# Two seven-product stages: four early quads run in pairs, and the second operand sum moved into the last head

## The chip, the cores and the metric

One core of one Trainium2 chip runs the whole program in one launch. The metric is device time in microseconds (us): the median of three runs of the kernel before is 1768.44 us (1766.1 to 1769.79). The trace is of a fourth execution of its own.

## The reference

One layer of a diffusion block on 1024 latent tokens of width 1024, with 256 context tokens, in float32. Two of its products carry the change: the latents times `w_in`, and the feed-forward's first product.

```python
h_lat = rmsnorm(x, norm1_g) * (1 + sc1) + sh1
u, v, q, k, vv, r, af, ab, ga, gb = split(h_lat @ w_in)
b_lat = gla(q, k, vv, af, ab, state of the context) normed * silu(r)   # 4 heads, forwards and backwards
a_lat = gelu(u) * (w_spatial mixing of layernorm(gelu(v)))
y = sigmoid(ga) * (a_lat @ w_branch_a) + sigmoid(gb) * (b_lat @ w_branch_b)
x = x + g1 * (y @ w_out)
h2 = rmsnorm(x, norm2_g) * (1 + sc2) + sh2
a, g = split(h2 @ w_ffn_in)
x = x + g2 * ((silu(g) * a) @ w_ffn_out)
return rmsnorm(x, final_norm_g)
```

## The kernel before, in words

**Products.** Every float32 operand is split into a high part (a cast on ACT to the reduced format fp32r) and a low part (raw minus high, on DVE). A product of two such operands is three matmuls of the parts (high by high, high by low, low by high) for each of its k blocks; `PASS` holds that order.

**Seven-product stages.** Blocks of columns of `w_in` (gb, u, r, ga) and of `w_ffn_in` are computed by a seven-product scheme on 2x2 blocks. The moving operands (tokens) are the blocks B11, B21, B22 and four sums T1 to T4 of blocks, computed once for a stage; the stationary ones (weights) are A11, A12, A22 and the sums S1 to S4. One **quad** is two column blocks of 128 for all 1024 tokens: seven products of 12 matmuls of 128x512, in the order A11 by B11 and A12 by B21 (`ahead_1`, `ahead_2`), then S3 by T3, S2 by T2, S1 by T1, A22 by T4, S4 by B22 (`others`). S3 and S2 accumulate in PSUM bank X, and A22 after them; S1 and S4 in bank Y. Between S3 and S2 ACT copies X into `q7` (L736), and the next product into X waits for that copy. After S2 DVE forms `u3` (L741), GpSimd subtracts `q7` from it (L742), DVE adds Y into `u3` (L744), and so on; `sink` applies the activation and stores. The latent stage has 16 quads, the feed-forward stage 22.

**Early quads.** `early_quads` runs the first two products of some quads before the sums T exist: they need only A11, A12, B11 and B21. In the latent stage these are quads 0 to 3 inside the last head (from `between`, which also forms T3 in `h_first`), and quads 4 and 5 after the head; in the feed-forward stage quads 0 to 3. Then `h_others` (latents) or `other_operands` (feed-forward) forms the sums on DVE, with the weights of quad 0 split between T2 and T1, and `run_quads` goes quad by quad: `weights_s` of one quad, then its five products.

**Weights.** `weights` (L689) loads one column block as a tile `wr` of 512 KB by a DMA from SyncE. `wr` comes from the pool `wraw`, which has 3 buffers, so a fourth load waits for the last reader of the first:

```python
wraw = ctx.enter_context(tc.tile_pool(name="wraw", bufs=3))
```

`weights_s` reads both column blocks (va, ga) of a quad: S3 = A11 - A21 (L700), S2 = A22 - S3 (L701), S1 = S2 + A11 (L702), S4 = A12 - S2 (L703, the last reader of va), splits S3 and S2 as one tile, S1 and S4 as another (`parts_of`, L637 cast, L638 low part), and splits A22 (L709, L710, the last reader of ga). In early quads L702 and L703 are on DVE, in later ones on GpSimd. The split of a first weight goes through `split_w` (L236 cast, L237 low part) and the pool `wspl` of 4 buffers.

**Order.** Each engine runs its queue strictly in order. A scheduler fixes the queues when the program is built; `pe` chains the matmuls of these stages in program order, so that PE never passes a product that waits.

**The last head.** `head` computes scores and masks, then for each of four pairs of chunks `outputs`: matmuls, a sum of squares on ACT, `rstd` (DVE L171, GpSimd L172), a scaling on ACT (L596); one step later `outputs_T`: four transposes on PE (L605) and two copies on DVE (L610).

## Time and profile before

| | us |
|---|---|
| median of three runs (lowest to highest) | 1768.44 (1766.1 to 1769.79) |
| profiled execution: its own time | 1771.97 |
| profiled execution: span from first to last instruction | 1770.2 |
| PE busy in the span | 1712.4 (97%) |
| DVE busy | 1138.8 (64%) |
| ACT busy | 668.5 (38%) |
| POOL (GpSimd) busy | 215.4 (12%) |

The profile gives busy time by engine, the time that each engine stood idle and what ended it, and the TensorE clock that was granted (1.00 is 2.4 GHz, 0.50 is 1.2 GHz). A matmul's row lasts 0.39 us, but the matmuls of a product overlap: the distance between two starts counts. The latent stage's stretch is 396 to 741 us, the feed-forward's 1108 to 1550 us.

### The profile page before, as it was taken

The numbers are of one execution on the slowest core, as the hardware profiler recorded it, in microseconds if no ns is written. First come the engines' busy times: TensorE is split into PE (matmuls) and PEld (weight loads), VectorE is DVE, ScalarE is ACT, GpSimd is POOL, SyncE is SP. The second block draws the span as 40 slices with busy tenths as digits, with TensorE's granted clock in tenths as the row PEclk, the third lists the DMA queues.
The fourth block names the chain that finished last, engine by engine and source line by source line (L and its number), as shares of the span: only waits on it lengthen the run. The fifth ranks groups of instructions, "written<-read, shape, count | busy, mean of one in ns | idle before, by whom it ended". The sixth has DMA issues, their size and how long they took to land.

```text
span 1770.2 us, 21603 instructions
## 1 busy us (share of the span) xinstructions
PE 1712.4 (97%) x8162; PEld 1407.5 (80%) x8162; DVE 1138.8 (64%) x1559; ACT 668.5 (38%) x974; POOL 215.4 (12%) x193
## 2 busy tenths in 40 slices
PE   8899999999899999999999999989999999999997
PEld 3887888888678888877888888768888888888886
DVE  7686595867865464277656745885545555466797
ACT  6663423323443434234322213533333333355343
POOL 2220000000112353000000000012122122000001
PEclk9999999999999999999999999989999999999999
DMA  9511234052354454387858951233222232377572
GB/s 339 156 37 36 85 118 179 24 179 60 113 155 133 129 179 125 124 293 260 262 190 308 321 191 74 70 116 98 77 90 83 75 92 84 127 242 277 180 270 99
DMA packets 219961, 267.89 MB, mean 151 GB/s; under 512 B 11920, under 2 KB 142032, under 8 KB 219856
## 3 DMA queue, kind: packets, MB, share of 16 engines
q1 hardware_dynamic: 219040, 265.08, 45.1%
q0 software_dynamic: 720, 1.40, 0.2%
q8 instruction: 64, 1.05, 0.2%
q14 instruction: 41, 0.34, 0.1%
q10 hardware_dynamic: 96, 0.02, 0.0%
HBM read 205.64 MB, written 60.82 MB: 151 GB/s over the span
## 4 chain that ended last, share of the span: by engine, by line
PE 79%; DVE 11%; DMA 4%; issue 3%; ACT 3%; POOL 1%; SPq 0%; DVEq 0%; ACTq 0%; POOLq 0%
PE m L716 20%; PE g L716 17%; PE m L273 13%; PE m L1283 5%; PE g L1283 5%; PE m L1166 5%; PE m L285 4%; PE g L538 2%; DVE s L638 1%; PE m L822 1%; DVE wlo L237 1%; DVE s L422 1%; PE g L822 1%; DMA s<-in_w_ada_dram 1%; PE g L1363 1%
## 5 line engine op out<-in xcount | busy, mean ns | idle before, releaser
L716 PE MATMUL m<-s,s 128*128 128x512 f32 x1320 | 313.5, 395 | 8.8 <-ACT q L736 3.8
L716 PEld LDWEIGHTS m<-s,s 128*128 128x128 f32 x1320 | 251.0, 191 | 65.1 <-ACT q L736 5.8
L273 PE MATMUL m<-s,whi 128*128 128x512 f32 (+1 forms) x832 | 252.3, 384 | 2.2 <-ACT s L990 1.5
L237 DVE TENSOR_TENSOR wlo<-wr,whi 128x1024 fp32r<-128x1024 f32 x92 | 112.4, 1224 | 194.2 <-ACT whi L236 194.0
L716 PE MATMUL g<-s,s 128*128 128x512 f32 x960 | 225.0, 391 | 9.0 <-ACT q L736 4.1
L716 PEld LDWEIGHTS g<-s,s 128*128 128x128 f32 x960 | 179.2, 188 | 51.6 <-ACT q L736 6.6
L273 PEld LDWEIGHTS m<-s,whi 128*128 128x128 f32 x832 | 154.0, 188 | 33.2 <-ACT s L990 2.4
L236 ACT CAST whi<-wr 128x1024 fp32r<-128x1024 f32 x92 | 96.5, 1051 | 214.1 <-PE m L273 107.9
L273 PE MATMUL m<-s,wlo 128*128 128x512 f32 (+1 forms) x416 | 158.9, 383 | 1.8 <-DVE wlo L237 1.8
L637 ACT CAST s<-s 128x1024 fp32r<-128x1024 f32 x98 | 102.4, 1052 | 134.4 <-DVE s L638 62.2
L638 DVE TENSOR_TENSOR s<-s,s 128x1024 fp32r<-128x1024 f32 x98 | 145.4, 1494 | 9.9 <-ACT s L637 6.0
L172 POOL TENSOR_TENSOR rstd<-rstd,nhalf 128x1 f32<-128x1 f32 (+2 forms) x43 | 29.1, 678 | 847.7 <-DVE rstd L171 847.6
L285 PE MATMUL m<-whi,s 128*128 128x256 f32 x640 | 126.0, 291 | 0.1
L716 PE MATMUL g<-s,whi 128*128 128x512 f32 x384 | 118.5, 390 | 0.0
L638 DVE TENSOR_TENSOR s<-wr,s 128x1024 fp32r<-128x1024 f32 x77 | 92.3, 1233 | 22.8 <-ACT s L637 22.1
L285 PEld LDWEIGHTS m<-whi,s 128*128 128x128 f32 x640 | 101.5, 192 | 4.2 <-issue 2.7
L742 POOL TENSOR_TENSOR q<-u,q 128x512 f32<-128x512 f32 x38 | 59.4, 1563 | 314.1 <-DVE u L741 150.3
L637 ACT CAST s<-wr 128x1024 fp32r<-128x1024 f32 x77 | 78.2, 1053 | 49.9 <-DMA wr<-wsT 25.3
L285 PE MATMUL m<-wlo,s 128*128 128x256 f32 x320 | 92.3, 289 | 2.6 <-DVE wlo L237 1.9
L273 PEld LDWEIGHTS m<-s,wlo 128*128 128x128 f32 x416 | 78.3, 188 | 16.6 <-DVE wlo L237 2.0
L1166 PE MATMUL m<-s,s 128*128 128x512 f32 x384 | 87.6, 390 | 0.0
L1166 PEld LDWEIGHTS m<-s,s 128*128 128x128 f32 x384 | 72.0, 188 | 14.9
(293 smaller groups left out, 2879.2 us busy)
## 6 DMA issues: line engine op xcount, KB each, us to landing
wr<-in_w_in_dram SPq DMA_DIRECT2D x82, 512.0 KB
s<-in_w_ada_dram SPq DMA_DIRECT2D x48, 512.0 KB
wr<-in_w_ffn_in_dram SPq DMA_DIRECT2D x48, 512.0 KB
wr<-actd SPq DMA_DIRECT2D x77, 256.0 KB
s<-in_w_ffn_out_dram SPq DMA_DIRECT2D x22, 512.0 KB
wsT<-s SPq DMA_DIRECT2D x44, 256.0 KB
wr<-wsT SPq DMA_DIRECT2D x44, 256.0 KB
wr<-in_w_ffn_out_dram SPq DMA_DIRECT2D x33, 256.0 KB
```

Source lines behind the costliest of these rows:

```text
L236: nc.scalar.copy(hi, raw)
L237: lo_sub[0] = nc.vector.tensor_sub(lo, raw, f(hi)).ins
L273: nc.tensor.matmul(ps, ws[a][:, k, :], get(b, k, t0, n), start=k == 0 and i == 0, stop=k == nk - 1 and i == 2)
L285: nc.tensor.matmul(ps[:, j, :], get(b, 4 * kh + k, (2 * tp + j) * P, P), ws[a][:, k, :], start=kh == 0 and j == 0 and k == 0 and i == 0, s ...
L538: r = nc.tensor.matmul(pkv[:, j, :], kt[:, j, :], vt(n), start=j == 0, stop=True, skip_group_check=True)
L637: nc.scalar.copy(hi, raw)
L638: nc.vector.tensor_sub(lo, raw, f(hi))
L716: pe(nc.tensor.matmul(ps, wts[a][:, k, :], mov[k // 2][b][:, k % 2, :], start=start and k == 0 and i == 0, stop=k == 3 and i == 2, skip_gr ...
L742: nc.gpsimd.tensor_sub(q7, u3, q7)
L822: pe(nc.tensor.matmul(banks[tt], op[mov][kp][b][:, kk, tt * P:(tt + 1) * P], wts[a][:, kk, :], start=start and kp == 0 and kk == 0 and i = ...
L1166: pe(nc.tensor.matmul(ps, yF.get(b, k, tt * P, P), wo[k // 2][a][:, k % 2, :], start=k == 0 and i == 0, stop=k == KT - 1 and i == 2))
L1283: pe(nc.tensor.matmul(banks[tt], o[b][:, 0, tt * P:(tt + 1) * P], o[a][:, 1, :], start=start and k == 0 and i == 0, stop=k == KH - 1 and i ...
```

## The change

Five things are changed. (1) `quad_pair` takes quads 0 and 1 together, then 2 and 3: the weights of both first, then each of the five products for both quads before the next product, with 4 PSUM banks for their X and Y. (2) In the latent stage quads 4 and 5 are no longer early: they run as every later quad does. (3) `weights_s` is a generator that splits S1 and S4 later, after S2's products; with GpSimd the sums S1, S4 come before the split of S3 and S2. (4) The sums T are a generator as well (`h_sums`, `f_sums`), stepped between the products of the first pair; T2 of the latents is formed in steps after each `outputs` of the last head, and the sums are formed in place. (5) T4 of the latents subtracts the tile that now holds T2.

```diff
@@ -616,6 +616,7 @@
                 outputs_T(jp - 1, ons[jp - 1])
+            step()
         for fo in range(2):
@@ -667,18 +668,27 @@
-    def other_operands(op, blk, after):
+    def in_place(op, dst, xs, ys):
+        for d, a, b in zip(dst, xs, ys):
+            getattr(nc.vector, op)(d, a, b)
+    def f_sums(op, blk):
...
-        dve = (nc.vector, nc.vector)
-        t3 = combined("tensor_sub", b22, b12, dve)
-        op["T3"] = moving(t3)
-        t2 = combined("tensor_add", t3, b11, dve)
-        op["T2"] = moving(t2)
-        after()
-        op["T1"] = moving(combined("tensor_sub", b12, b11, dve))
-        op["T4"] = moving(combined("tensor_sub", b21, t2, dve))
+        t = combined("tensor_sub", b22, b12, (nc.vector, nc.vector))
+        op["T3"] = moving(t)
+        yield
+        in_place("tensor_add", t, t, b11)
+        op["T2"] = moving(t)
+        yield
+        in_place("tensor_sub", b12, b12, b11)
+        op["T1"] = moving(b12)
+        yield
+        in_place("tensor_sub", b21, b21, t)
+        op["T4"] = moving(b21)
+        yield
...
+        yield
@@ -695,20 +705,38 @@
-        nc.vector.tensor_sub(s32[:, 0], a11, a21)
-        nc.vector.tensor_sub(s32[:, 1], a22, s32[:, 0])
-        eng.tensor_add(s14[:, 0], s32[:, 1], a11)
-        eng.tensor_sub(s14[:, 1], a12, s32[:, 1])
-        for t, names in ((s32, ("S3", "S2")), (s14, ("S1", "S4"))):
+        def split(t, names):
...
+        def sums14():
+            eng.tensor_add(s14[:, 0], s32[:, 1], a11)
+            eng.tensor_sub(s14[:, 1], a12, s32[:, 1])
+        nc.vector.tensor_sub(s32[:, 0], a11, a21)
+        nc.vector.tensor_sub(s32[:, 1], a22, s32[:, 0])
+        if eng is nc.gpsimd:
+            sums14()
+        split(s32, ("S3", "S2"))
+        if eng is nc.vector:
+            sums14()
...
+        yield
+        split(s14, ("S1", "S4"))
+        yield
+    def whole(*gens):
+        for _ in zip(*gens):
+            pass
@@ -761,19 +794,33 @@
-    def run_quads(op, todo, quads, hook=None):
+    def quad_pair(op, todo, quads, at, sums=None):
+        ws = [weights_s(*weights(*todo[at + i][:2]), quads[at + i]["ops"], nc.vector) for i in range(2)]
+        steps = [others(quads[at + i], op, todo[at + i][2]) for i in range(2)]
+        def run(gens):
+            for g in gens:
+                next(g)
+        run(ws)
+        run(steps)
+        for i in range(4):
+            if sums:
+                next(sums)
+            if i == 1:
+                run(ws)
+            run(steps)
+    def run_quads(op, todo, at, hook=None):
...
-            if fi < len(quads):
-                if fi:
-                    weights_s(*weights(w, cols), quads[fi]["ops"], nc.vector)
-                others(quads[fi], op, sink)
-            else:
+            if fi >= at:
...
-                weights_s(va, ga, q["ops"], nc.gpsimd)
+                whole(weights_s(va, ga, q["ops"], nc.gpsimd))
...
-                others(q, op, sink, lambda: (ahead_2(q, op), hook and hook(fi)))
+                whole(others(q, op, sink, lambda: (ahead_2(q, op), hook and hook(fi))))
@@ -872,26 +919,28 @@
-    def in_place(op, dst, xs, ys):
-        for d, a, b in zip(dst, xs, ys):
-            getattr(nc.vector, op)(d, a, b)
-    def h_first(op):
+    def h_sums(op):
...
-        return b22, b12
-    def h_others(op, b22, b12, after):
-        b11 = h_raw(0, 0)
+        yield
+        b11, op["T2"] = [], []
+        for i, (hi, lo) in enumerate(h_moving(0, 0)):
+            b11.append(slot([P, 2, 512]))
+            nc.vector.tensor_add(b11[i], f(hi), f(lo))
+            yield
+            nc.vector.tensor_add(b22[i], b22[i], b11[i])
+            yield
+            op["T2"].append(parts_of(b22[i]))
+            yield
...
-        in_place("tensor_add", b11, b11, b22)
-        op["T2"] = moving(b11)
-        after()
...
+        yield
...
-        in_place("tensor_sub", b21, b21, b11)
+        in_place("tensor_sub", b21, b21, b22)
...
+        yield
@@ -972,19 +1021,22 @@
-            sums.extend(h_first(h_op))
+            next(sums)
...
+        t2_steps = [2, 2, 1, 1, 0]
+        def step():
+            if h + 1 == HEADS:
+                for _ in range(t2_steps.pop(0)):
+                    next(sums)
...
-        head(h, *now, v, between)
+        head(h, *now, v, between, step)
...
-    p1t = slot([P, 2, 512])
-    quads.extend(early_quads(h_op, todo, 4, gbank, [p1t[:, i, :] for i in range(2)]))
-    h_others(h_op, *sums, lambda: weights_s(*weights(*todo[0][:2]), quads[0]["ops"], nc.vector))
@@ -1006,7 +1058,9 @@
-    run_quads(h_op, todo, quads)
+    quad_pair(h_op, todo, quads, 0, itertools.chain((None,), sums, (None,)))
+    quad_pair(h_op, todo, quads, 2)
+    run_quads(h_op, todo, 4)
@@ -1268,10 +1322,14 @@
-    quads = early_quads(f_op, todo, 0, gbank, None, lambda: block_T(f_blk, xns[4:], 1, bank, f_scale, f_shift))
-    quads += early_quads(f_op, todo, 2, gbank)
-    other_operands(f_op, f_blk, lambda: weights_s(*weights(*todo[0][:2]), quads[0]["ops"], nc.vector))
-    run_quads(f_op, todo, quads, f_hook)
+    p1s = four()
+    quads = early_quads(f_op, todo, 0, gbank, p1s[:2], lambda: block_T(f_blk, xns[4:], 1, bank, f_scale, f_shift))
+    quads += early_quads(f_op, todo, 2, gbank, p1s[2:])
+    sums = f_sums(f_op, f_blk)
+    next(sums)
+    quad_pair(f_op, todo, quads, 0, sums)
+    quad_pair(f_op, todo, quads, 2)
+    run_quads(f_op, todo, 4, f_hook)
```

What the scheduler makes of it, at three places (L721, L722, L718, L719, L730, L639 and L744 of after are L700, L701, L702, L703, L710, L638 and L716 of before). The first is PE's queue in the latent stage, from the last transposes of the last head (`on`) on. Before, `m_...`/`g_4104` and `g_4118` are the A products of quads 4 and 5, `g_4219` and `g_4220` are X and Y of quad 0:

```order
L605 MATMUL g_4075<-ident,on_4043 128x128 x4
L605 MATMUL g_4082<-ident,on_4066 128x128
L716 MATMUL g_4104<-s_921,whi_4094 128x512
...
L716 MATMUL g_4104<-s_921,wlo_4095 128x512
...
L716 MATMUL g_4118<-s_921,whi_4100 128x512
...
L716 MATMUL g_4219<-s_3959,s_4182 128x512
...
L716 MATMUL g_4219<-s_4164,s_4182 128x512
...
L716 MATMUL g_4220<-s_4193,s_4186 128x512
...
L716 MATMUL g_4219<-s_4207,s_4190 128x512
```

After, `g_4143` is X of quad 0 and `g_4163` X of quad 1:

```order
L605 MATMUL g_4085<-ident,on_4052 128x128 x4
L605 MATMUL g_4096<-ident,on_4076 128x128 x4
L744 MATMUL g_4143<-s_3959,s_4121 128x512
...
L744 MATMUL g_4143<-s_3959,s_4122 128x512
...
L744 MATMUL g_4163<-s_3959,s_4134 128x512
...
L744 MATMUL g_4163<-s_3959,s_4135 128x512
...
L744 MATMUL g_4143<-s_4039,s_4121 128x512
...
L744 MATMUL g_4163<-s_4039,s_4134 128x512
```

The 48 matmuls of quads 4 and 5 that stood behind the transposes are gone from here, and S3 by T3 of quad 0 follows the transposes directly; S3 by T3 of quad 1 stands before S2 by T2 of quad 0.

The second place is DVE's queue in the latent stage, where the weights of the first quads are combined (`wr` are the raw column blocks). Before, quad 0:

```order
L700 TENSOR_TENSOR s_4176<-wr_4172,wr_4174 128x512
L701 TENSOR_TENSOR s_4176<-wr_4174,s_4176 128x512
L702 TENSOR_TENSOR s_4177<-s_4176,wr_4172 128x512
L703 TENSOR_TENSOR s_4177<-wr_4172,s_4176 128x512
L638 TENSOR_TENSOR s_4183<-s_4176,s_4182 128x1024
L638 TENSOR_TENSOR s_4187<-s_4177,s_4186 128x1024
L710 TENSOR_TENSOR s_4190<-wr_4174,s_4190 128x512
```

After, quad 0 reads `wr_4109` and `wr_4111`, quad 1 `wr_4113` and `wr_4115`:

```order
L721 TENSOR_TENSOR s_4117<-wr_4109,wr_4111 128x512
L722 TENSOR_TENSOR s_4117<-wr_4111,s_4117 128x512
L639 TENSOR_TENSOR s_4122<-s_4117,s_4121 128x1024
L718 TENSOR_TENSOR s_4118<-s_4117,wr_4109 128x512
L719 TENSOR_TENSOR s_4118<-wr_4109,s_4117 128x512
L730 TENSOR_TENSOR s_4127<-wr_4111,s_4127 128x512
L721 TENSOR_TENSOR s_4130<-wr_4113,wr_4115 128x512
L722 TENSOR_TENSOR s_4130<-wr_4115,s_4130 128x512
L639 TENSOR_TENSOR s_4135<-s_4130,s_4134 128x1024
```

The load of `wr_4115`, the fourth tile of the pair, goes into the buffer of `wr_4109`, whose last reader is L719; before, the weights of the second quad stood behind the sums T1 and T4. In SyncE's queue the first three loads of the pair stand before the head's last two stores, `wr_4115` behind them.

The third place is DVE's queue at the start of the feed-forward stage: L237 is the low part of the first weights of quads 2 and 3. Before:

```order
L646 TENSOR_TENSOR s_9181<-s_9040,s_9038 128x1024
L638 TENSOR_TENSOR s_9184<-s_9179,s_9183 128x1024
L237 TENSOR_TENSOR wlo_9116<-wr_9113,whi_9115 128x1024
L638 TENSOR_TENSOR s_9188<-s_9181,s_9187 128x1024
L237 TENSOR_TENSOR wlo_9122<-wr_9119,whi_9121 128x1024
L646 TENSOR_TENSOR s_9191<-s_9179,s_8823 128x1024
...
L700 TENSOR_TENSOR s_9207<-wr_9203,wr_9205 128x512
L701 TENSOR_TENSOR s_9207<-wr_9205,s_9207 128x512
...
L638 TENSOR_TENSOR s_9214<-s_9207,s_9213 128x1024
```

After (`wr_9186` and `wr_9188` are quad 0's column blocks):

```order
L664 TENSOR_SCALAR s_9037<-m_9080,mod_1181,mod_1180 128x512
L237 TENSOR_TENSOR wlo_9113<-wr_9110,whi_9112 128x1024
L237 TENSOR_TENSOR wlo_9119<-wr_9116,whi_9118 128x1024
L647 TENSOR_TENSOR s_9174<-s_9036,s_9034 128x1024
...
L673 TENSOR_TENSOR s_9034<-s_9034,s_8820 128x1024
L639 TENSOR_TENSOR s_9179<-s_9174,s_9178 128x1024
...
L721 TENSOR_TENSOR s_9194<-wr_9186,wr_9188 128x512
L673 TENSOR_TENSOR s_9174<-s_9174,s_8820 128x1024
L722 TENSOR_TENSOR s_9194<-wr_9188,s_9194 128x512
...
L673 TENSOR_TENSOR s_9035<-s_9035,s_8821 128x1024
L639 TENSOR_TENSOR s_9199<-s_9194,s_9198 128x1024
```

Both L237 now stand ahead of the sums, and four sums for T1 and T2 stand before the low part of S3 and S2 of quad 0 (`s_9199`).

## Rows read from the trace of the kernel before

**Rows 1.** The page's first part: busy us, share of the span, instructions.
```profile
PE 1712.4 (97%) x8162; PEld 1407.5 (80%) x8162; DVE 1138.8 (64%) x1559; ACT 668.5 (38%) x974; POOL 215.4 (12%) x193
```

**Rows 2.** Windows: stretch and its length, busy us of each engine, clock, DMA.
```profile
400.00:500.00 100.00, 90.89 (x414) 72.04 (x413) 79.31 (x115) 42.52 (x72) 8.25 (x7) 1.00 0.36 101
1100.00:1200.00 100.00, 91.16 (x384) 72.41 (x383) 81.35 (x93) 44.80 (x56) 13.44 (x10) 0.93 0.31 95
1300.00:1400.00 100.00, 100.00 (x443) 82.83 (x442) 55.61 (x67) 31.80 (x42) 19.80 (x16) 1.00 0.27 84
```

**Rows 3.** PE's timeline: start, length, instruction, count, idle before and its releaser.
```profile
444.50 0.33 PE L605 MATMUL g<-ident,on 128*128 128x128 f32 x1 [2.04 <-ACT on L596]
...
550.66 0.61 PE L716 MATMUL m<-s,whi 128*128 128x512 f32 x2
...
1134.12 2.88 PE L716 MATMUL m<-s,s 128*128 128x512 f32 x12
...
1157.85 4.63 PE L716 MATMUL m<-s,s 128*128 128x512 f32 x10 [2.65 <-DVE s L638]
...
1205.57 0.62 PE L716 MATMUL g<-s,whi 128*128 128x512 f32 x2
...
1208.29 2.88 PE L716 MATMUL m<-s,s 128*128 128x512 f32 x12
```

**Rows 4.** Windows of 10 us, columns as in rows 2 (the granted clock is third last).
```profile
450.00:460.00 10.00, 7.29 (x31) 5.41 (x30) 9.93 (x11) 5.36 (x7) 0.00 (x0) 1.00 0.06 7
1150.00:1160.00 10.00, 7.19 (x19) 5.49 (x20) 7.96 (x12) 3.84 (x5) 0.00 (x0) 0.69 0.32 96
1160.00:1170.00 10.00, 9.28 (x27) 6.86 (x27) 6.82 (x9) 3.00 (x4) 0.96 (x1) 0.63 0.40 115
```

**Rows 5.** PE's groups, both stages: last, idle before and its releasers.
```profile
PE g L716 <- ACT q L736: 4.1, 6, 0.7
PE m L716 <- ACT q L736: 3.8, 4, 1.7
```

**Rows 6.** Timelines of DVE and ACT where quad 0's weights are combined.
```profile
442.50 0.48 DVE L610 TENSOR_SCALAR s<-g,pcol 128x256 f32<-128x256 f32 x1 [1.97 <-PE g L605]
...
445.66 0.88 DVE L610 TENSOR_SCALAR s<-g,pcol 128x256 f32<-128x256 f32 x2 [2.10 <-PE g L605]
...
455.61 0.68 DVE L700 TENSOR_TENSOR s<-wr,wr 128x512 f32<-128x512 f32 x1
456.33 0.69 DVE L701 TENSOR_TENSOR s<-wr,s 128x512 f32<-128x512 f32 x1
457.05 0.69 DVE L702 TENSOR_TENSOR s<-s,wr 128x512 f32<-128x512 f32 x1
...
458.26 2.42 DVE L638 TENSOR_TENSOR s<-s,s 128x1024 fp32r<-128x1024 f32 x2
...
457.05 1.05 ACT L637 CAST s<-s 128x1024 fp32r<-128x1024 f32 x1 [2.62 <-DVE s L701]
...
1123.17 1.05 ACT L236 CAST whi<-wr 128x1024 fp32r<-128x1024 f32 x1 [0.72 <-PE g L716]
```

**Rows 7.** Loads of a column block: SyncE's issue, and DVE's reader that waits for it.
```profile
476.00 0.38 SPq L689 DMA_DIRECT2D wr<-in_w_in_dram  x1
...
480.65 0.69 DVE L700 TENSOR_TENSOR s<-wr,wr 128x512 f32<-128x512 f32 x1 [1.20 <-DMA wr<-in_w_in_dram]
...
1156.09 0.37 SPq L689 DMA_DIRECT2D wr<-in_w_ffn_in_dram  x1
...
1160.45 0.69 DVE L700 TENSOR_TENSOR s<-wr,wr 128x512 f32<-128x512 f32 x1 [0.92 <-DMA wr<-in_w_ffn_in_dram]
```

**Rows 8.** GpSimd's L742 with and without DVE at work, and DVE beside it.
```profile
468.88 3.25 POOL L742 TENSOR_TENSOR q<-u,q 128x512 f32<-128x512 f32 x1 [24.93 <-DVE u L741]
...
545.02 1.29 POOL L742 TENSOR_TENSOR q<-u,q 128x512 f32<-128x512 f32 x1
...
500.40 1.66 DVE L702 TENSOR_TENSOR s<-s,wr 128x512 f32<-128x512 f32 x1
```

More of the change, by code (lines that the diff above doesn't have):

```diff
@@ L490, in head_products, with head @@
         return v
-    def head(h, qq, kk, dec, v, between):
+    def head(h, qq, kk, dec, v, between, step):
         def vt(n):
@@ L882, in h_first @@
         op["T3"] = moving(b22)
-        return b22, b12
-    def h_others(op, b22, b12, after):
-        b11 = h_raw(0, 0)
+        yield
[3 more added lines that the diff above has]
+            nc.vector.tensor_add(b11[i], f(hi), f(lo))
+            yield
+            nc.vector.tensor_add(b22[i], b22[i], b11[i])
+            yield
+            op["T2"].append(parts_of(b22[i]))
+            yield
         in_place("tensor_sub", b12, b12, b11)
-        in_place("tensor_add", b11, b11, b22)
-        op["T2"] = moving(b11)
-        after()
         op["T1"] = moving(b12)
+        yield
         b21 = h_raw(1, 0)
-        in_place("tensor_sub", b21, b21, b11)
+        in_place("tensor_sub", b21, b21, b22)
         op["T4"] = moving(b21)
+        yield
     rd, ud, gbd, gad = proj("rd"), proj("ud"), proj("gbd"), proj("gad")
@@ L963, in block_kernel @@
     v = head_products(0, *ahead[:2])
-    quads, sums, p1s = [], [], []
+    quads, sums, p1s = [], h_sums(h_op), []
     for h in range(HEADS):
```

## The prediction

> **What bounds the kernel now.** I read the page's busy times first: PE is busy for 97% of the span [rows 1], so a change that leaves the matmuls alone can only win or lose what PE loses in waits. The reader is to see there that no other engine is near that. Next the windows of 100 us, for where PE is not full: nearly all loss lies in two of them, 400 to 500 and 1100 to 1200 us, while in 1300 to 1400 PE never stops [rows 2]. These are the starts of the two seven-product stages. Then PE's timeline for what a product costs: between two products without a wait, 1205.57 and 1208.29, lie 2.72 us for 12 matmuls, 0.227 each [rows 3].
>
> With that the loss of each start can be counted. Latents, from the last transposes of the last head (444.50) to the first product of quad 6 (550.66): 106.2 us [rows 3], for 4 early products of quads 4 and 5 and 30 products of quads 0 to 5, 34 x 2.72 = 92.5, and 0.4 of transposes. Lost: 13.3 us. Feed-forward, from the first S3 product (1134.12) to the first product of quad 4 (1205.57): 71.45 us [rows 3] for 20 products, 54.4. Lost: 17.0 us. Together 30.3 us, which is all that the two starts can give back.
>
> What the loss consists of: ten waits of PE for ACT's copy `q7`, 7.9 us [rows 5], one a quad; waits for low parts of sums and weights, 2.65 us at most [rows 3]; and the clock. In 1150 to 1170 us it was granted at 0.69 and 0.63 [rows 4], that is, for part of that time it stood at 1.2 instead of 2.4 GHz: 19 + 27 matmuls took 7.19 + 9.28 = 16.5 us of busy time where 46 x 0.227 = 10.4 do. That is 6.0 of the 17.0 us.
>
> **The change part by part.** The sum is made on the profiled execution's own time, 1771.97 us (span 1770.2), which lies 3.5 us above the median of the runs, 1768.44.
>
> Removed: the copy waits of the first four quads, since the other quad's product (2.72 us) now covers the copy. With quads 4 and 5 no longer early, theirs go too: all ten, -7.9 us. Removed as well: the 10.9 us of early products of quads 4 and 5 behind the transposes. They are not lost work (they run later), but they were the cover for the sums and quad 0's weights, 446 to 456 us. Two column loads fall away, which nobody waited for. Four sums S1, S4 (quads 4, 5) move to GpSimd at 1.3 us instead of 0.6, as every later quad has them beside a busy PE: nothing.
>
> Latents after, each wait of PE in order:
> (a) T2's steps in the last head. DVE idled about 2 us before each pair of L610, 1.97 and 2.10 for two of them [rows 6], and each `rstd` is now queued behind at most two operations of 1.2 us. They fit almost; between 0 and 2.4, I take 1.2.
> (b) From the transposes' end (445.1) to S3 of quad 0: L610 ends at 446.5, then L700, L701 to 447.9, the cast 1.05 [rows 6], so 449.0. PE stands for 3.9.
> (c) The third matmul needs the low part, 1.22 us later (half of the 2.42 for two) [rows 6]; two matmuls cover 0.45: 0.8.
> (d) S3 of quad 1. Its second column block is the fourth tile in a pool of three, so its load starts when L703 of quad 0 is done. The low part ends at 450.2, L702 and L703 take 1.2, the load 4.4 to 4.65 from issue to reader (476.00 to 480.65, 1156.09 to 1160.45) [rows 7], I take 4.5; then L700 and L701 1.4, cast 1.1: 458.4. PE ends quad 0's product at 450.2 + 10 x 0.227 = 452.5, and next in its queue is this very product: 5.9. Products that could run (S2 by T2 of quad 0 has all it needs) stand behind it.
> (e) Its low part: 0.8 again.
> (f) T4. From the low part of quad 1's S3 to T4's, DVE has nine wide operations at 1.2 (half of the 2.42) and six at 0.6, 14.4 us; PE has ten matmuls and four products to run, 13.2, and up to one more before the low part is missed: the two nearly balance. But GpSimd's L742 shares something with DVE: 3.25 us with DVE at work against 1.29 without, and a DVE operation beside it takes 1.66 instead of 0.69 [rows 8]. Twice that is 2 us. Between 0.5 and 3, I take 2.5.
> (g) S3 of quad 3. Its fourth load waits for L703 of quad 2, which stands on DVE behind the adds that wait for A22 of quad 1. PE covers with three products, 8.2; the chain is 0.8 + 0.6 + 4.5 + 2.0 + 1.1 = 9.0, plus 0.8 for the low part: 1.5.
> Sum: 16.6, against 13.3.
>
> Feed-forward after: (a) quad 0 starts late. L237 of quad 3 waits for a cast that cannot start before 1123.17 [rows 6], so it ends at 1125.4, and now all sums stand behind it: eight wide and two half operations, 9.6 + 1.2, and quad 0's low part, 1.2: 1137.4. The third matmul was possible at 1134.6: 2.8. (b) quad 1's fourth load: issued at 1138.6, landed 1143.0, S3 ready at 1145.5, PE free at 1139.7: 5.8. (c) low parts of S3 and T2: 0.8 + 0.5. (d) quad 3: as in the latents, but on DVE the last sums and the products of `sink` (L1259) stand before L703 of quad 2, some 4 us more than above: 3.7 + 0.8. Sum 14.4, against 17.0 - 6.0 without the clock.
>
> The clock. After, PE has 12 matmuls between standing still for 3.9 and for 5.9 us, far less than in the stretch in which it fell before, 7.19 of 10 us busy with waits of up to 2.65 [rows 3, 4]. So I expect the low clock in both stages. Quad 0's slow matmuls are hidden in the wait for quad 1's load, quad 1's 12 are not: 2.7 and a little of S2, 3 in the latents; 4 in the feed-forward, whose later gap is longer. Bounds: 0, and 6.0 each as measured. The Trainium skill says of this, under "TensorE: Matmul & The Clock Gate", section "HAM oscillation — how this bites in real kernels", that bursts of matmuls parted by waits for loads restart at the lower clock each time. The trace agrees for 1150 us and not for 450 to 460, where PE was busy 7.29 of 10 us and the clock stayed at 1.00 [rows 4]; by the rule alone both pairs of each stage would pay, which is the third rival.
>
> Of the shared something in (f) the Trainium skill, "SBUF — State Buffer", section "Terms", says that VectorE and GpSimd take one port pair in turn, each for a whole instruction. The rows agree (1.66 us), and by that rule (f) is 2.5 rather than the 0.5 that the durations alone give.
>
> Total: 16.6 + 14.4 + 7 = 38.0 us lost after, 30.3 before: +7.7 us. 1771.97 + 7.7 = 1779.7; less 3.5, 1776.1 for the median, as the runs of before lie.
>
> **Rivals.** First, the pairing gives what it can: quad 1's and quad 3's fourth columns are there in time. For it: three of the four are loaded long before, and DMA is at 31 to 36% in these windows [rows 2]. Against: three buffers, and the reader L703 that frees the first runs after quad 0 has started. Then (d) shrinks to DVE's own 1.4 in each stage, the later gaps go, and no wait is long enough for the clock: -4.5 - 1.5 - 4.4 - 4.5 - 7 = -22, 16.0 lost, 14.3 us faster: 1754.1. It decides if the first column is freed before S3 of quad 0 starts.
>
> Second, the waits come as above but the clock does not fall, as it did not at 450 to 460 us [rows 4]: 31.0 lost against 30.3, 1769.1, no change. Against it: PE's gaps there were 2 us, now they are 4 to 6.
>
> Third, the clock stays low for as long as before in each stage, 6.0 instead of 3 and 4, and loads beside two stores of 512 KB (the head's `bd`) take 1.5 us longer for each of the four late columns: 5 + 6 = 11 more, 1787; half of it, 1781.6.
>
> **How the numbers follow.** My forecast 50%, its own range 1771 to 1780 from (a) and (f) of the latents and 2 us of the clock. First rival 8%, second 17%, third 25%. The range for 8 in 10 leaves out the first rival and the end of the third: 1766 to 1786. About 0.2%, 3.5 us, is what a measurement of this kernel can tell from no change. Faster than that needs the first rival, 0.08; within it lie the second rival and the low end of the forecast, 0.18; slower 0.74.
>
> **What would show it.** Right: PE stands for 5 to 7 us before the second S3 product in both stages, released by ACT's cast, DVE's subtraction before it released by a DMA; no wait for the `q7` copy in quads 0 to 5; PEclk below 1.00 near 450 to 470 us, where it was 1.00. Wrong: the load of quad 1's second column issued before L703 of quad 0; a clock of 1.00 in the latents; or DVE still late at T4 for more than 3 us, so that the sums and not the load bound the pair.

## The result, and the profile after

The changed kernel takes 1781.23 us (median of 4 runs, 1779.58 to 1781.95) against 1768.61 us (4 runs of before beside it): a ratio of 1.0072, 95% interval 1.0055 to 1.0089, or 12.6 us more. Slower was the forecast, and the time lies in the range, but it is 5 us above the predicted 1776.1. The profiled execution of after has an own time of 1781.87 us and a span of 1780.0, 9.8 more than the span of before.

The page's first part, busy us, share of the span and instructions, answers to [rows 1]:

```profile
PE 1720.5 (97%) x8162; PEld 1411.6 (79%) x8162; DVE 1141.3 (64%) x1555; ACT 664.0 (37%) x974; POOL 218.9 (12%) x197
```

The matmuls are as many as before, 8162, but by the page's count PE was busy with them for 8.1 us more, out of 9.8: most of what is lost shows as longer busy time for the same number of matmuls, and PE's idle time is nearly what it was. Next the windows of the profile after, with the columns of [rows 2] and [rows 4]. The first three answer to [rows 2], the others to [rows 4]:

```profile
400.00:500.00 100.00, 86.78 (x383) 68.69 (x381) 78.16 (x114) 40.88 (x71) 7.04 (x6) 0.93 0.31 90
1100.00:1200.00 100.00, 88.91 (x387) 71.49 (x386) 78.15 (x91) 46.49 (x59) 10.12 (x8) 0.91 0.26 79
1300.00:1400.00 100.00, 100.00 (x439) 81.78 (x438) 55.93 (x63) 31.07 (x41) 20.38 (x16) 1.00 0.27 85
450.00:460.00 10.00, 5.56 (x14) 3.69 (x14) 5.06 (x7) 4.94 (x8) 0.00 (x0) 0.67 0.58 166
1150.00:1160.00 10.00, 8.11 (x24) 6.03 (x25) 7.95 (x9) 6.81 (x9) 0.00 (x0) 0.66 0.40 108
1180.00:1190.00 10.00, 6.40 (x19) 4.39 (x18) 7.25 (x11) 4.89 (x6) 0.00 (x0) 0.73 0.58 180
```

The clock in 450 to 460 us, 1.00 before, is now 0.67, and a second stretch at a low clock has come at 1180 to 1190. The middle of the feed-forward, 1300 to 1400, still has PE busy for 100%, but with 439 matmuls in place of 443. So PE is not full there in the sense that counts, and the change costs something far from the places at which it was costed.

PE's timeline after, start, length, instruction, count, and the idle time before it with its releaser. These rows answer to [rows 3]:

```profile
446.01 0.91 PE L605 MATMUL g<-ident,on 128*128 128x128 f32 x4 [2.14 <-ACT on L596]
450.29 4.98 PE L744 MATMUL g<-s,s 128*128 128x512 f32 x12 [3.37 <-ACT s L638]
...
459.38 16.63 PE L744 MATMUL g<-s,s 128*128 128x512 f32 x61 [4.11 <-ACT s L638]
...
477.34 14.04 PE L744 MATMUL g<-s,s 128*128 128x512 f32 x59 [1.33 <-DVE s L639]
...
555.82 0.62 PE L744 MATMUL m<-s,whi 128*128 128x512 f32 x2
...
1141.70 0.73 PE L744 MATMUL m<-s,s 128*128 128x512 f32 x2 [0.86 <-ACT s L638]
...
1144.03 3.93 PE L744 MATMUL m<-s,s 128*128 128x512 f32 x10 [1.59 <-DVE s L639]
...
1151.85 30.25 PE L744 MATMUL m<-s,s 128*128 128x512 f32 x120 [3.90 <-ACT s L638]
...
1185.67 27.66 PE L744 MATMUL m<-s,s 128*128 128x512 f32 x108 [3.56 <-ACT s L638]
...
1213.17 0.61 PE L744 MATMUL g<-s,whi 128*128 128x512 f32 x2
```

450.29 is S3 of the latents' quad 0 and 459.38 S3 of quad 1: PE stands 4.11 us before it, released by ACT's cast. 1151.85 and 1185.67 are S3 of quads 1 and 3 of the feed-forward, with 3.90 and 3.56. The same matmul opens quad 6 of the latents at 555.82 (550.66 in [rows 3]) and quad 4 of the feed-forward at 1213.17 (1205.57).

What stands behind the 4.11 us is read on DVE and on SyncE (SPq is its DMA queue), in the same window:

```profile
452.01 0.68 DVE L719 TENSOR_TENSOR s<-wr,s 128x512 f32<-128x512 f32 x1
...
456.83 0.69 DVE L721 TENSOR_TENSOR s<-wr,wr 128x512 f32<-128x512 f32 x1 [3.53 <-DMA wr<-in_w_in_dram]
...
452.73 1.01 SPq L699 DMA_DIRECT2D wr<-in_w_in_dram  x2
```

L719 is the last reader of quad 0's first column (L703 before). The fourth load is issued at 452.73, when L719 is through, and is there for L721 of quad 1 at 456.83, 4.1 us later (4.4 and 4.65 in [rows 7]). DVE waited 3.53 us for it. This is the chain that the prediction described. In the feed-forward the same load is a smaller part: DVE waits 1.25 us for it at 1149.30 and 1.59 us at 1182.59.

The marks, the same matmul in three profiles (the second profile of before is the last run of this study):

| start of | before | before, second profile | after |
|---|---|---|---|
| last transposes, latents | 444.50 | 444.50 | 446.01 |
| quad 6, latents | 550.66 | 550.78 | 555.82 |
| first product behind the latents' quads | 741.15 | 741.18 | 747.30 |
| block transposes, feed-forward | 1114.22 | 1114.09 | 1120.85 |
| first S3, feed-forward | 1134.12 | 1133.99 | 1141.70 |
| quad 4, feed-forward | 1205.57 | 1201.26 | 1213.17 |
| first product behind the feed-forward's quads | 1550.11 | 1545.80 | 1560.22 |
| span | 1770.2 | 1765.9 | 1780.0 |

After stands 1.5 us behind at the head's end, of which 0.7 was there at 410 us already, before anything that the change touches. It stands 5.2 behind at quad 6, 7.6 at the first S3 and at quad 4 of the feed-forward, and 9.8 at the end. Against the second profile of before it is 11.9 behind at quad 4 and 14.1 at the end.

### The profile page after: what moved, and what is told of

The parts are those of the page before. It is cut to its first block, busy times and chain, and to the rows that moved or that the text cites. A ratio compares the mean times of both kernels' runs of the same rounds, so it can differ in the third digit from the quotient of the medians.

```text
span 1780.0 us, 21582 instructions
## 1 busy us (share of the span) xinstructions
PE 1720.5 (97%) x8162; PEld 1411.6 (79%) x8162; DVE 1141.3 (64%) x1555; ACT 664.0 (37%) x974; POOL 218.9 (12%) x197
## 4 chain that ended last, share of the span: by engine, by line
PE 77%; DVE 11%; DMA 5%; ACT 3%; issue 3%; POOL 1%; SPq 0%; DVEq 0%; POOLq 0%; ACTq 0%
PE m L744 20%; PE g L744 17%; PE m L273 11%; PE m L1341 5%; PE g L1341 5%; PE m L1220 5%; PE m L285 4%; DMA s<-in_w_ffn_out_dram 2%; PE g L538 2%; DVE s L639 1%; DMA wr<-in_w_in_dram 1%; DVE s L422 1%; PE m L869 1%; PE g L869 1%; PE g L1421 1%
## 5 line engine op out<-in xcount | busy, mean ns | idle before, releaser
L744 PE MATMUL m<-s,s 128*128 128x512 f32 x1320 | 315.8, 397 | 10.0 <-ACT s L638 8.3
L744 PEld LDWEIGHTS m<-s,s 128*128 128x128 f32 x1320 | 250.5, 191 | 69.2 <-ACT s L638 9.6
L237 DVE TENSOR_TENSOR wlo<-wr,whi 128x1024 fp32r<-128x1024 f32 x92 | 113.2, 1233 | 198.6 <-ACT whi L236 198.4
L744 PE MATMUL g<-s,s 128*128 128x512 f32 x960 | 228.9, 396 | 10.2 <-ACT s L638 8.2
L744 PEld LDWEIGHTS g<-s,s 128*128 128x128 f32 x960 | 181.6, 191 | 53.5 <-ACT s L638 9.3
L639 DVE TENSOR_TENSOR s<-s,s 128x1024 fp32r<-128x1024 f32 x98 | 150.4, 1544 | 36.1 <-PE g L744 19.9
L638 ACT CAST s<-s 128x1024 fp32r<-128x1024 f32 x98 | 101.2, 1048 | 78.2 <-PE m L744 28.2
L744 PE MATMUL g<-s,whi 128*128 128x512 f32 x352 | 108.4, 389 | 0.0
L639 DVE TENSOR_TENSOR s<-wr,s 128x1024 fp32r<-128x1024 f32 x77 | 92.2, 1231 | 23.3 <-ACT s L638 23.3
L638 ACT CAST s<-wr 128x1024 fp32r<-128x1024 f32 x77 | 78.2, 1052 | 50.0 <-DMA wr<-wsT 17.8
```

The lines of the kernel that those rows point to most:

```text
L237: lo_sub[0] = nc.vector.tensor_sub(lo, raw, f(hi)).ins
L638: nc.scalar.copy(hi, raw)
L639: nc.vector.tensor_sub(lo, raw, f(hi))
L744: pe(nc.tensor.matmul(ps, wts[a][:, k, :], mov[k // 2][b][:, k % 2, :], start=start and k == 0 and i == 0, stop=k == 3 and i == 2, skip_gr ...
```

## The experiments

Each run is compared with before on the same chip. The changed kernel, run again beside some of them, gave 1779.68 us, a ratio of 1.0071, interval 1.0058 to 1.0083, and differences from the changed kernel below are differences of ratios to this one. By the two intervals each such difference is uncertain by about 3 us.

> The changed kernel itself once more, beside the other three on their chip, for the differences between them. All theories: 1.0072 times the kernel before, within 0.0017, and TensorE's waits before the second S3 of each stage again about 4 us.

Its waits before the second S3 are 3.91 us in the latents and 3.67 and 3.40 in the feed-forward, near the 4.11, 3.90 and 3.56 of the first profile.

**The fourth column in a buffer of its own** (`last=slot` for the pair's second quad):

```
-            t = raw_w([P, KT, P])
+            t = (last if last and i else raw_w)([P, KT, P])
...
-        ws = [weights_s(*weights(*todo[at + i][:2]), quads[at + i]["ops"], nc.vector) for i in range(2)]
+        ws = [weights_s(*weights(*todo[at + i][:2], last=slot if i else None), quads[at + i]["ops"], nc.vector) for i in range(2)]
```

> The changed kernel, but in each pair the fourth weight column (the second one of the pair's second quad) is loaded into a buffer of its own in the large pool, so that it no longer waits for a buffer of the pool of three. Theory (the late fourth column is the main loss of the change): the subtraction at the start of quads 1 and 3 of both stages no longer stands behind a load, TensorE's waits before the second S3 shrink from 4.1 us (latents) and 3.9 and 3.6 us (feed-forward) to 0 to 2 us each, and some of the low-clock stretches behind them go (1 to 3 us each): 8 to 14 us less than the changed kernel, 1767 to 1773 us. Rival (VectorE's and ScalarE's queue of sums and casts sets these waits whatever the load does): under 3 us less, the waits stay above 3 us and are put down to the cast with VectorE busy ahead of it.

Measured: 1772.87 us, ratio 1.0032 (1.0019 to 1.0044), 0.39% or 6.9 us less than the changed kernel: the theory's direction, short of its 8 to 14. PE's timeline of this run, the latents' start, and one row of DVE:

```profile
450.34 5.11 PE L744 MATMUL g<-s,s 128*128 128x512 f32 x12 [3.37 <-ACT s L638]
455.81 0.73 PE L744 MATMUL g<-s,s 128*128 128x512 f32 x2 [0.37 <-ACT s L638]
457.07 13.43 PE L744 MATMUL g<-s,s 128*128 128x512 f32 x58 [0.53 <-DVE s L639]
...
473.79 0.50 PE L744 MATMUL g<-s,s 128*128 128x512 f32 x1 [3.29 <-ACT s L638]
475.52 24.74 PE L744 MATMUL g<-s,s 128*128 128x512 f32 x95 [1.23 <-DVE s L639]
...
467.42 3.44 DVE L918 TENSOR_TENSOR s<-s,s 128x1024 f32<-128x1024 f32 x2
```

The wait before S3 of quad 1 fell from 4.11 to 0.37 us. But two waits, 3.29 us at 473.79 for the cast and 1.23 for the low part, have come at T4's product, where the changed kernel had 1.33 in all. Its sum of B21's parts (L918) starts only at 467.42 on DVE and takes 3.44 us for two, 1.72 each, beside GpSimd's work as in [rows 8]. So the load was the bound, and behind it stood DVE's queue at T4, the prediction's term (f), which took most of the latents' gain: quad 6 starts 1.2 us earlier than after, at 554.66. In the feed-forward the waits on the cast fell from 8.3 to 5.2 us in all: 2.70 and 1.62 are left before the second S3, with no load to wait for, behind other work on DVE. So the late column is only a part of the wait there.

**The order of the later quads' splits as before** (S1 and S4 ahead of A22 where GpSimd forms the sums):

```
+        if eng is nc.gpsimd:
+            split(s14, ("S1", "S4"))
         both = slot([P, 2, 4, P], F32R)
...
-        split(s14, ("S1", "S4"))
+        if eng is nc.vector:
+            split(s14, ("S1", "S4"))
```

> The changed kernel, but in the later quads (fifth and on, both stages) the weights' sums are split in the order of the kernel before: S1 and S4 ahead of A22. The four early quads keep the changed order. Theory (A22's split on VectorE, which waits for ScalarE's copy, stands ahead of the addition that reads bank Y, and S4 by B22 waits for that addition: about 0.14 us in each of 28 later quads, 4.3 and 2.0 us of waits on that addition in the weight loads): 3 to 5 us less than the changed kernel, 1776 to 1778 us, and no weight load waits for that addition in the later quads. Rival (the slow growth over the later quads is the clock or the DMA): less than 1 us of difference.

Measured: 1775.14 us, ratio 1.0043 (1.003 to 1.0056), 5.0 us less than the changed kernel. First DVE in a later quad of before, then the same quad in the changed kernel, then this run:

```profile
1276.88 0.68 DVE L744 TENSOR_TENSOR u<-m,u 128x512 f32<-128x512 f32 x1
...
1282.91 0.68 DVE L710 TENSOR_TENSOR s<-wr,s 128x512 fp32r<-128x512 f32 x1
```

```profile
1282.76 2.33 DVE L639 TENSOR_TENSOR s<-s,s 128x1024 fp32r<-128x1024 f32 x1 [0.17 <-ACT s L638]
1285.82 0.69 DVE L730 TENSOR_TENSOR s<-wr,s 128x512 fp32r<-128x512 f32 x1 [0.73 <-ACT s L729]
1286.43 0.68 DVE L774 TENSOR_TENSOR u<-m,u 128x512 f32<-128x512 f32 x1
...
1287.17 2.59 PEld L744 LDWEIGHTS m<-s,s 128*128 128x128 f32 x12 [0.29 <-DVE u L774]
```

```profile
1278.15 2.33 DVE L639 TENSOR_TENSOR s<-s,s 128x1024 fp32r<-128x1024 f32 x1 [0.17 <-ACT s L638]
1280.40 0.68 DVE L777 TENSOR_TENSOR u<-m,u 128x512 f32<-128x512 f32 x1
```

L774 (L744 before, L777 in this run) adds bank Y to u3. In the changed kernel the low part of A22 (L730) stands ahead of it on DVE and waits 0.73 us for ACT; before, that low part (L710) comes 6 us behind the addition. S4 by B22 writes bank Y next, and the weight load of its first matmul waits 0.29 us for L774. By the waits of PE's weight loads over the whole of the changed kernel this adds up to 6.3 us, 22 times. The first two rows are the changed kernel, the third this run after 560 us:

```profile
PEld m L744 <- DVE u L774: 4.3, 15, 0.3
PEld g L744 <- DVE u L774: 2.0, 7, 0.3
```

```profile
PEld g L747 <- DVE u L777: 0.2, 1, 0.2
```

The rival falls: with the old order the wait is gone and so is the time. A part of a weight load's wait is hidden behind the matmul that still runs, so PE itself lost less than 6.3. From quad 4 to the first product behind the feed-forward's quads before takes 344.5 us, the changed kernel 347.1 and this run 344.5; from quad 6 to the end of the latents' quads they take 190.5, 191.5 and 190.5. So the trace shows 3.5 us in these later quads, and the old order gives all of it back. The rest of the 5.0 lies within the uncertainty.

**Both edits.**

> The changed kernel with both edits of the two runs before: the fourth column in a buffer of its own, and the kernel before's order of splits in the later quads. Theory: the two losses stand in different places and add, 11 to 18 us less than the changed kernel, 1763 to 1770 us, about the kernel before or a little under it. Rival (one loss hides in the other, or the clock takes the gain back): the gain is at most the larger of the two alone.

Measured: 1768.15 us (11 runs), ratio 1.0005 (0.9996 to 1.0014). That is 11.7 us less than the changed kernel, and 6.9 + 5.0 is 11.9: the two losses are separate and add up (so close an agreement is chance, at 3 us of uncertainty), and together they are as much as the change costs against before. That balance has two sides. Against the second profile of before, quad 6 of the latents starts 2.1 us late in this run (552.85), and in the feed-forward the stretch from the block transposes to quad 4 is 1.6 us shorter (85.6 against 87.2).

**A product of filler in the feed-forward's waits.**

```
+        if fill:
+            product(Y, fill["S3"], op["T3"], True)
         product(X, ops["S3"], op["T3"], True)
```

> The changed kernel with one more product (S3 of the pair's first quad by T3 again, 12 matmuls into a bank that a later product overwrites) ahead of the second S3 in both pairs of the feed-forward: work that the kernel does not need, put where TensorE waits 3.9 and 3.6 us. Theory (the wait costs twice, once as idle time and once as the low clock that follows it): the 12 matmuls, 2.7 us at the high clock, lie in the wait, and the stretches at the low clock after 1150 and 1184 us shrink or go: 2 to 7 us less than the changed kernel in spite of the added work, 1774 to 1779 us. Rival (the clock falls for the earlier waits near 1143 us and the filler runs at the low clock, 5.4 us): 2 to 4 us more than the changed kernel, 1783 to 1785 us.

Measured: 1777.25 us, ratio 1.0058 (1.0044 to 1.0072), 2.3 us less than the changed kernel, with 24 matmuls more. The intervals overlap, so the runs alone do not show the sign. The trace does, as far as one profile goes: from the feed-forward's first S3 to its quad 4 this run takes 69.8 us with 24 matmuls more, and the three profiles with the same kernel text there and no filler take 71.5 (the changed kernel, twice) and 71.4 (the run without steps in the last head). The windows:

```profile
1150.00:1160.00 10.00, 8.65 (x36) 6.34 (x35) 8.96 (x10) 8.51 (x10) 0.56 (x1) 1.00 0.38 105
1180.00:1190.00 10.00, 8.04 (x28) 5.88 (x27) 7.58 (x9) 5.38 (x7) 0.00 (x0) 0.83 0.55 161
```

In 1150 to 1160 us PE was granted 1.00 instead of 0.66 and ran 36 matmuls instead of 24. In 1180 to 1190 it was 0.83 and 28 instead of 0.73 and 19. So with the wait filled the clock behind it was higher, and work that nobody needs paid for itself in this profile. The run with the old order leaves the waits unfilled too and took 70.6 us for the stretch, so only 0.8 us of the gain lies outside the spread of these four profiles.

**The feed-forward alone** (before up to the latents' end, then the pairs of the changed kernel with a fourth column of their own; later quads as before):

```
+    quad_pair(f_op, todo, quads, 0, sums)
+    quad_pair(f_op, todo, quads, 2)
+    run_quads(f_op, todo, quads, f_hook, 4)
```

> The kernel before up to and with the latents; only the feed-forward has the changed form: its four early quads in pairs, product by product, with the fourth column of a pair in a buffer of its own, and the later quads as before. Theory (with its column in time the pairing is worth something in the feed-forward, where T2, T1 and T4 are formed beside products, and costs something in the latents: with both edits TensorE's marks stood 0.8 us late before the feed-forward's start and 5.0 us early after its four quads): 5 to 7 us less than the kernel before, 1760 to 1762 us. Rival (those 5.8 us came from the shifted latents, or from the clock's chance course): within 2 us of the kernel before.

Measured: 1766.41 us (11 runs), ratio 0.9993 (0.9984 to 1.0002): a miss. In its profile the mark at quad 4 stands 5.9 us ahead of the profile of before shown here, and yet the runs hardly differ. The second profile of before says why:

**Before once more.**

> The kernel before once more, for a second profile: the profiled execution shown of it took 1771.97 us, above every one of its 40 other runs, 1765.5 to 1770.05 us. If the difference lies in the feed-forward's start (where the shown profile has a stretch at a clock of 0.69 and 0.63), the pairing's gain there, 5.6 us against that profile, is in truth smaller, as the run of the feed-forward alone says (0.07 per cent of difference): the marks of TensorE after the four quads stand 3 to 5 us earlier than in the shown profile. Rival (the difference lies elsewhere, as in the loads of the first part): the marks stand alike at the end of the four quads and differ before the latents or after the feed-forward.

Measured: 1767.64 us, the span 1765.9. The windows of this second profile, and quad 4 of the feed-forward on PE:

```profile
1150.00:1160.00 10.00, 7.51 (x24) 5.25 (x24) 9.16 (x14) 3.75 (x5) 0.00 (x0) 0.83 0.43 132
1160.00:1170.00 10.00, 9.28 (x42) 7.68 (x42) 9.29 (x12) 5.03 (x7) 1.61 (x1) 1.00 0.44 132
...
1201.26 0.62 PE L716 MATMUL g<-s,whi 128*128 128x512 f32 x2
```

Where the first profile has 0.69 and 0.63 with 19 and 27 matmuls [rows 4], this execution was granted 0.83 and 1.00 with 24 and 42. Quad 4 starts at 1201.26 instead of 1205.57, and these 4.31 us are the whole difference of the two spans, 4.3. Against this profile the quad-4 mark of the feed-forward alone (1199.68) is 1.6 us ahead, and its span (1764.3) as well. The profile that the prediction was made on had an uncommonly long low clock in just the stretch that the change rebuilds.

**B21's sum early, on VectorE, then on GpSimd.** In the kernel with both edits the sum that T4 needs is formed with T3's sums, ahead of the last head's outputs:

```
         op["T3"] = moving(b22)
+        b21 = h_raw(1, 0)               # second run: h_raw(1, 0, nc.gpsimd)
         yield
...
-        b21 = h_raw(1, 0)
         in_place("tensor_sub", b21, b21, b22)
```

> The kernel with both edits, and in the latents B21's sum of its two parts, which T4 needs, is formed with T3's sums ahead of the last head's outputs instead of behind T2's products. Theory (what bounds the latents' first pair once its columns are in time is T4: the wait of 3.7 us near 473 us, behind the two sums of 1.7 us each on VectorE beside GpSimd's subtraction, and the low clock behind that wait): that wait falls under 1 us and the clock of 470 to 480 us rises: 3 to 6 us less than with both edits, 1762 to 1765 us. Rival (T4 is bound by the chain of products and evictions before it, or the two sums make the head's outputs late by their 2.4 us): within 1.5 us of the kernel with both edits.

> As the run with B21's sum formed early, but on GpSimd, which has nothing to do in the last head, so that VectorE's queue there carries none of it. Theory (T4's wait is VectorE's queue, and the early sum on VectorE gave the gain back in the head, where the transposes' marks moved from 0.5 us to 5.9 us late): the head ends within 1.5 us of the kernel with both edits, the wait of 3.7 us near 473 us falls under 1 us, and the kernel takes 3 to 5 us less than with both edits, 1763 to 1765 us. Rival (the two engines share a way to the memory, and GpSimd's two sums of about 2 us each slow VectorE in the head by as much): the head's end moves by 2 us or more, and the time is within 1.5 us of the kernel with both edits.

Measured: on VectorE 1767.12 us, ratio 0.9999 (0.999 to 1.0008), the same as without. On GpSimd 1762.54 us, ratio 0.9973 (0.9963 to 0.9983): 5.1 us faster than before, and the fastest of all. PE in the head and behind it, on VectorE first, then on GpSimd with GpSimd's two sums:

```profile
450.52 0.91 PE L605 MATMUL g<-ident,on 128*128 128x128 f32 x4 [2.14 <-ACT on L596]
455.81 6.46 PE L747 MATMUL g<-s,s 128*128 128x512 f32 x14 [4.38 <-ACT s L638]
```

```profile
446.09 1.19 PE L605 MATMUL g<-ident,on 128*128 128x128 f32 x4 [2.13 <-ACT on L596]
...
451.66 6.20 PE L747 MATMUL g<-s,s 128*128 128x512 f32 x14 [4.38 <-ACT s L638]
458.39 51.89 PE L747 MATMUL g<-s,s 128*128 128x512 f32 x226 [0.53 <-DVE s L639]
...
387.72 2.40 POOL L921 TENSOR_TENSOR s<-s,s 128x1024 f32<-128x1024 f32 x1 [23.18 <-DVE s L982]
394.79 2.37 POOL L921 TENSOR_TENSOR s<-s,s 128x1024 f32<-128x1024 f32 x1 [4.67 <-PE g L986]
```

In both T4's wait is gone (from 458.39 on PE runs 226 matmuls with no wait in the second). The scheduler also moved T4's subtractions (L673) ahead in both, into the head and in front of quad 0's S2, so the gain is that of the sums and the subtractions together. On VectorE the last transposes came at 450.52, with GpSimd at 446.09. On VectorE the head lost what T4 gained, as the rival said, by 5.4 us and not its 2.4. GpSimd was idle in the head, ran its sums at 387.72 and 394.79, long before the outputs, and the head did not move by more than 1.0 us against the kernel with both edits, 445.13. The first S3 did come 2.2 us later than there (451.66 against 449.41), with one of the subtractions ahead of it on DVE, and still quad 6 starts 4.7 us earlier (548.20). Whether the same sums on GpSimd would help the kernel before, without the pairs, was not run.

**No steps in the last head** (changed kernel, T2 formed behind the pair's S3 products):

```
-        t2_steps = [2, 2, 1, 1, 0]
+        t2_steps = [0, 0, 0, 0, 0]
...
-    quad_pair(h_op, todo, quads, 0, itertools.chain((None,), sums, (None,)))
+    quad_pair(h_op, todo, quads, 0, itertools.chain(itertools.islice(sums, 5, 6), sums, (None,)))
```

> The changed kernel without the steps in the last head: T2's sums and splits all stand behind the pair's S3 products, ahead of S2 by T2. Theory (the steps cost the head under 1 us and take 7 us of VectorE's work off the latents' start): the last transposes end 0.7 us earlier, S2 by T2 of the first quad waits for T2, and the kernel takes 3 to 8 us more than the changed kernel. Rival (T2 would have lain beside the S3 products, whose end is late anyway for the fourth column): within 1.5 us of the changed kernel, or faster by the head's 0.7 us.

Measured: 1784.79 us, ratio 1.0099 (1.0086 to 1.0113), 5.0 us more than the changed kernel, inside the theory's 3 to 8. PE's timeline:

```profile
445.71 0.47 PE L605 MATMUL g<-ident,on 128*128 128x128 f32 x1 [1.93 <-ACT on L596]
445.83 1.20 PE L744 MATMUL g<-s,s 128*128 128x512 f32 x2
446.83 0.84 PE L605 MATMUL g<-ident,on 128*128 128x128 f32 x3
...
458.67 0.50 PE L744 MATMUL g<-s,s 128*128 128x512 f32 x1 [2.60 <-ACT s L638]
...
463.40 0.80 PE L744 MATMUL g<-s,s 128*128 128x512 f32 x1 [0.97 <-ACT s L638]
...
479.15 0.50 PE L744 MATMUL g<-s,s 128*128 128x512 f32 x1 [2.73 <-ACT s L638]
```

New waits stand at T2's product, 458.67 (2.60 us) and 463.40 (0.97), and the one at T4's has grown, at 479.15 (2.73). The theory's 0.7 us of the head did not come: one of the last four transposes runs at 445.71, the other three at 446.83, in the changed kernel all at 446.01. Nor was the freed room left empty: the scheduler put quad 0's weights into it (its last sum, L719, runs at 441.67), and the first S3 starts at 445.83 in place of 450.29. So the run weighs T2 in the head against quad 0's weights in the head, and T2 there is worth 5 us more.

## Why the prediction was right, and where it was not

**The mechanism is shown at the latents.** The change replaces ten short waits for a copy by a few long ones: S3 of a pair's second quad stands behind a load that the pool of three holds back (in the feed-forward behind the load in part, and behind other work on DVE for the rest). The marks that the prediction named came, with 4 in place of 5 to 7 us: PE's long waits before the second S3 in both stages are released by ACT's cast, DVE's subtraction before it by a DMA, of the waits for the copy [rows 5] none is left at the starts, and the clock near 450 us fell to 0.67. Giving that one load a buffer takes 6.9 us away. The first rival put columns in time at 22 us less; that was much too high, since T4 stood next in line (4.5 us in two waits) and the clock still fell. The third rival, at half its size 1781.6, comes nearest to the time, but only one of its two halves was there: the late column took 4.10 us from issue to reader, not 1.5 more, while the low clock of the feed-forward cost nearly its 6.0 (below).

**Sizes at the latents.** (a) was put at 1.2 us; the last transposes are 0.8 late, 1.5 less the 0.7 that was there before, but the run without the steps did not win it back, so that it is the steps' cost is not shown. (b) 3.9: 3.37; the prediction counted from 445.1, where the last transposes of before start, and they end at 445.6. (d) 5.9: 4.11. From S3 of quad 0 to S3 of quad 1 the chain itself was 9.4 in the prediction (449.0 to 458.4) and is 9.09 (450.29 to 459.38). What shortened the idle time is the low clock: quad 0's 12 matmuls show as a row of 4.98 us in place of 2.88 [rows 3], hidden in the wait, as was said. (f) 2.5: 1.33 in the changed kernel, 4.5 once the load was out of its way, so the late load hid a part of it. (g) 1.5: 0.74 and 0.53, two waits at 492.12 and 493.37. Together the latents' start was forecast at +6.3 and came out at 4.5, the 5.2 of the marks less 0.7.

**The feed-forward's start** was forecast at +1.4: 14.4 + 4 lost after, 17.0 before. Against the profile that the sum was made on, it was +1.0 (7.6 at quad 4, 6.6 at its block transposes, which start at 1114.22 and 1120.85 in the two traces): (a) 2.8, measured 0.86 and 1.59; (b) 5.8, measured 3.90; (d) 3.7, measured 3.56. The clock was put at 4 and cost 5.8: 120 and 108 matmuls took 30.25 and 27.66 us, where at 0.227 each they take 27.4 and 24.7. So shorter waits and a dearer clock nearly cancel. But the 17.0 held 6.0 of clock, and the second profile of before has 4.3 us less there. The step that failed is the last one of the sum: "less 3.5, 1776.1 for the median, as the runs of before lie". The 3.5 us by which the profile lay above the median was carried over to after as if it were spread over the span. It lay in the feed-forward's low clock, which the change replaces by its own, so it should not have been taken off: the forecast without that step is 1779.7, and the measured median 1781.23. That after's own profile lies only 0.6 us above its median agrees with this.

**The term that was missing** is the order of the splits in every later quad. The prediction has no term for it: its "nothing", "as every later quad has them beside a busy PE", is the price of the sums S1, S4 of quads 4 and 5, and that A22's low part comes ahead of the splits of S1 and S4 in all later quads was not costed. The added wait on ACT (0.73 us) stands on DVE ahead of the addition that frees bank Y, and so PE waits after all. The old order took 5.0 us off by the runs, of which the trace ties 3.5 to the later quads, 1.0 in the latents and 2.5 in the feed-forward. With the 3.5 that was taken off for the profile it is what the forecast left out.

The sum put right, by the marks against the second profile: 4.3 (latents' start) + 5.2 (feed-forward's start) + 3.6 (later quads, 1.1 and 2.5) + 0.7 from the first part = 13.8 of the 14.1 us between the spans. The medians differ by 12.6 to 12.8; after's profile lies 0.6 above its own.

That the time fell into the range is in part luck. The forecast's own band, 1771 to 1780, was missed by 1 us. The latents' start came out 1.8 us cheaper than forecast, the later quads 3.5 dearer, and 3.5 was taken off that should have stayed.

**What stays open**: why the clock of before stayed low for long in one execution and not in the other. The waits ahead of it were alike, 2.65 us at 1157.85 in the first [rows 3] and 2.48 in the second. The filler was profiled once, so how much of the higher clock behind it is the filler's and how much this variation is open too.

## What to carry to other kernels

A reordering that takes short waits away is worth no more than the latest of the operands that it now needs at once: count the buffers that the loads of such a group take, and then look for what stands second (here T4's sums, which an idle engine could form far ahead). When code is moved into a shared helper, every caller's order moves: a wait of 0.7 us on an engine that is only half busy held up PE's weight loads 22 times in the 30 later quads, because a bank was freed behind it. And before a profiled execution's excess over the median is subtracted from a forecast, a second profile must show where it lies.

## What the runs showed of the hardware

Two executions of the same kernel differ by 4.3 us, nearly all through the granted clock of one stretch, 0.69 and 0.63 in one, 0.83 and 1.00 in the other. After waits of 3.4 to 4.4 us the clock of 450 to 460 us was 0.67, and 0.66 in the run with GpSimd's sum, where PE then ran with no wait but one of 0.53 us; behind the 1.6 us waits of the kernel with both edits it was 0.78 in one stretch and 1.00 in another:

```profile
450.00:460.00 10.00, 7.77 (x21) 5.27 (x22) 7.28 (x10) 5.22 (x7) 0.00 (x0) 0.66 0.54 154
```

```profile
1140.00:1150.00 10.00, 7.80 (x25) 5.64 (x24) 8.72 (x10) 5.02 (x7) 0.00 (x0) 0.78 0.56 157
1170.00:1180.00 10.00, 7.85 (x34) 5.88 (x33) 8.86 (x13) 5.59 (x7) 0.00 (x0) 1.00 0.68 197
```

Where the low clock comes can't be told from the length of a single wait in these rows.

The Trainium skill, "TensorE: Matmul & The Clock Gate", section "HAM oscillation — how this bites in real kernels", has bursts between waits for loads restart at the lower clock. The filler's windows (0.66 to 1.00, 24 to 36 matmuls) agree with it; behind the wait of 1.6 us for a cast, with 1.00 after it, nothing of the kind shows.
